# Seven block products in chunks 1 to 12 of a squared-ReLU MLP, with buffers of their own for the weights of its two products

## The chip, the cores and the metric

One core of one Trainium2 chip runs the whole program. The metric is the device time of one execution in microseconds (us); lower is better. A profile is one execution of its own, taken by the hardware profiler, with its own time beside its span. Engines: PE is TensorE's matmuls, PEld its weight loads, DVE VectorE, ACT ScalarE, POOL GpSimd, SP SyncE, which here only issues DMAs.

## The reference

One layer of a causal decoder with 256 rows of 1024 features in float32: an RMSNorm and a joint input projection; a gated convolution branch and a sparse attention branch; cross attention over 256 memory tokens; an MLP with squared ReLU; a final RMSNorm. The part that matters here:

```
h = h + _cross_attention(_rmsnorm(h, norm_x_g[l]), _rmsnorm(mem, norm_mem_g[l]), wx_q[l], wx_kv[l], wx_o[l])
hf = _rmsnorm(h, norm_ffn_g[l]) @ w_ff1[l]          # (256, 1024) @ (1024, 4096)
h = h + jnp.square(jax.nn.relu(hf)) @ w_ff2[l]      # (256, 4096) @ (4096, 1024)
return _rmsnorm(h, norm_final_g)
```

## The kernel before

Every large product is made in three matmuls of a rounded float32 format: high part times high part, high times low, low times high. So each weight block that arrives by DMA is split: ScalarE copies it to its high part (`hi`), VectorE subtracts that from the block and writes the low part (`lo`). The same is done with the activations.

The MLP runs over 16 chunks of 256 hidden features. For chunk i, f1 (`first`, line 1256) makes the hidden values in two halves of 128 features, each 24 matmuls of 256 columns, or, in the wide form, 8 of 512 and 8 of 256. The ReLU and the square follow on ScalarE, then the hidden rows are split into `fs` (its high and low parts), the stationary side of f2. In the program, chunk c's f2 stands with chunk c+2's f1: half of f1, half of f2, the other half of f1, the rest of f2. Chunks 0 to 12 (JOINED is 13) are accumulated in common banks; the last three make their products at the very end, row half by row half.

A chunk's f2 is a 2x2 block product: two row halves of 128 and two halves of the 256 features by two halves of the 1024 columns. It takes eight block products of three 512-wide matmuls each, or, in the chunks listed in SEVEN (line 60), seven: then sums of the weight quarters (`sums`) and differences of the hidden quarters (`fn`) are needed. The weight side has four parts: `left`, `last`, `outer`, `inner`. VectorE makes the sums and all the low parts. The f1 that stands beside chunk c's f2 is wide if c isn't listed, chunk 5 excepted, and so is the f1 of chunks 0 and 1.

The order on each engine is that of the program text; nothing is reordered. A few queues in the program set it: `high_jobs` holds the splits still to come, in the order of use; `split_high` (ScalarE's copy) and `split_low` (VectorE's subtraction) take the next one each time a weight is used, at most HALVES (6) ahead. Generators (`activation`, the row turning) go one step further at each `tick`. Weights are loaded by SP in the order of STREAM (line 34), each 1 MB block into the next of three `raw` buffers. `load` is called when the last low part of a block is written, so the three buffers serve f1 and f2 in turn. In four f1 chunks (BY_HALVES) the load is issued as two halves. Between the loads SP also issues 16 copies that turn the residual from features to rows (`h_rm`).

The names that the prediction's steps touch: `load` (line 164), `seven` (line 214), `split_high` and `split_low` (lines 273 to 285), `activation` (line 1164), `Hidden` (line 1195), `seventh` and `first` (lines 1250 to 1264). The helper at line 80 records all matmuls and all VectorE instructions, so the names of the tiles tell them apart.

Of the kernel before, what the change touches and what calls it, by code (L numbers as in the profile page):

```python
# [59 lines left out]
SEVEN = (2, 3, 4, 6, 7, 8, 9, 10, 11, 12)  # L60
JOINED = 13
BY_HALVES = tuple(("f1", i) for i in (4, 5, 6, 7))
# [52 lines left out]
def block_kernel(ctx, tc, x, xt, mem, memt, wst, wki, vecs, convw, gout, out):  # L115
# [45 lines left out]
    nload = [0]  # L161
    high_jobs, low_jobs = [], []

    def load(parts=1):
        if nload[0] >= len(STREAM):
            return
        c = nload[0]
        nload[0] += 1
        key = STREAM[c]
        raw = t8(f"raw{c}", F32, (P, N_CHUNK)) if c in EARLY else raws.tile([P, N_CHUNK], F32, tag="raw", name=f"raw{c}")  # L170
        n = KT * NK if key[0] == "ki" else N_CHUNK
        parts = 2 if key in BY_HALVES else parts
        src = wki if key[0] == "ki" else wst[INDEX[key]]
        for q in range(parts):
            ns = slice(q * n // parts, (q + 1) * n // parts)
            nc.sync.dma_start(raw[:, ns], src[:, ns])
        if key in WHOLE:
            whole[key] = raw.rearrange("p (k n) -> p k n", k=2 * KT)
            return
        if key[0] == "f2" and key[1] in SEVEN:  # L180
# [8 lines left out]
        if key[0] == "f2" and key[1] < JOINED:

            at = [j.key for j in high_jobs].index(("f1", key[1] + 2, 1))
            first = len(jobs) // 2
            high_jobs[at:at] = jobs[:first]
            jobs = jobs[first:]
        if key == ("f1", JOINED + 2):

            at = [j.key for j in high_jobs].index(("f2", JOINED - 1, "inner"))
            high_jobs[at:at] = jobs[:1]
            jobs = jobs[1:]
        high_jobs.extend(jobs)  # L200
# [12 lines left out]

    def seven(key, c, raw):

        b = raw.rearrange("p (k h n) -> p k h n", k=2, h=2)
        flat = raw.rearrange("p (j n) -> p j n", j=4)
        sums = []

        def outer():  # L220
            sums.append(t8(f"sums{c}", F32, (P, 4, 512)))
            dve.tensor_tensor(out=sums[0][:, 0:2, :], in0=flat[:, 0:4:3, :],
                              in1=flat[:, 1:2, :].to_broadcast([P, 2, 512]), op=ALU.add)

        def inner():
# [4 lines left out]
        def stage(name, src_of, n, before=None):  # L230
            def high():
                src = src_of()
                if before:
# [16 lines left out]
            return Stage((*key, name), high, before, not before)  # L250

        return [stage("left", lambda: b[:, :, 0, :], 2), stage("last", lambda: flat[:, 3:4, :], 1),
                stage("outer", lambda: sums[0][:, 0:2, :], 2, outer), stage("inner", lambda: sums[0][:, 2:4, :], 2, inner)]

    def high(key, c, raw, ns, q, last):
        n = ns.stop - ns.start
# [183 lines left out]
    zero_r = cst.tile([P, 512], F32R, name="zero_r")  # L440
# [9 lines left out]
    ki2 = cst.tile([P, S], F32, name="ki2")  # L450
# [191 lines left out]
    bias = [cst.tile([P, P * (qb + 1)], F32, name=f"bias{qb}") for qb in range(2)]  # L642
# [22 lines left out]
    def index_scores():  # L665
# [497 lines left out]

    def activation(c, ct, ps, t, sh, sl):
        if ps.shape[1] == S:
            act(t[:, ct, :], ps, AF.Relu)  # L1166
        else:
            yield from merge(t[:, ct, :], ps)
            yield
            act(t[:, ct, :], t[:, ct, :], AF.Relu)  # L1170
# [272 lines left out]
```

## Time and profile before

| | |
|---|---|
| time, median of 3 runs | 505.51 us (505.5 to 505.59) |
| the profiled execution's own time | 505.25 us |
| its span | 503.5 us |
| granted TensorE clock | 0.998 |
| PE busy | 493.6 us |
| DVE busy | 459.9 us |
| ACT busy | 349.1 us |
| f1 of chunk 0 begins | 323.05 us |
| last product begins to end | 480.6 to 497.3 us |

A line of the timeline gives start, duration, engine, line of the program, operation, tiles written and read, shape, and in brackets the idle time just before it and who ended it. Durations of VectorE's and ScalarE's instructions overlap their successors' a little, and matmuls are pipelined, so the cost of one in a row of many is read from start to start. In a line of the waits stand the total, the number and the longest.

### The profile page before, as it was taken

The page shows a single profiled execution, that of the slowest core. Times are in us where ns is not written, and L with a number is a line of the kernel's source. Part 1 is how long each engine was busy: PE and PEld are TensorE (multiplying, and loading weights), DVE is VectorE, ACT ScalarE, POOL GpSimd, SP SyncE. Part 2 cuts the span into 40 slices and gives each one's busy share as a digit, 9 for nine tenths or more (in the row PEclk, how much of TensorE's full clock was granted, in tenths as well). Part 3 has the DMA queues.
Part 4 walks back from the last instruction along what each step waited for, and adds up shares of the span by engine and source line. Part 5 has one row for each costly group of instructions (what it writes and reads, how often), then busy time and mean ns, then how long its engine had stood idle before and what let it go on. Part 6 is the DMA issues. An engine that isn't in the chain of part 4 may idle for free.

```text
span 503.5 us, 8292 instructions
## 1 busy us (share of the span) xinstructions
PE 493.6 (98%) x3119; PEld 444.1 (88%) x3119; DVE 459.9 (91%) x858; ACT 349.1 (69%) x639; POOL 31.6 (6%) x49
## 2 busy tenths in 40 slices
PE   7999999999999999999999999999999999999995
PEld 5999998888888888888889999988989899988984
DVE  5999999999999799999988986888999899999994
ACT  7657777788656676668756667586777677777832
POOL 2002212221021100000000000000000000000000
PEclk9999999999999999999999999999999999999999
DMA  8949678899787744345645454368855645544602
GB/s 312 381 184 280 185 191 261 226 246 262 225 265 215 191 148 144 119 158 197 246 169 218 175 174 161 127 192 214 239 181 184 235 159 206 221 178 168 251 1 84
DMA packets 27225, 100.36 MB, mean 199 GB/s; under 512 B 10656, under 2 KB 11552, under 8 KB 17200
## 3 DMA queue, kind: packets, MB, share of 16 engines
q1 hardware_dynamic: 23120, 92.90, 53.4%
q0 software_dynamic: 3632, 6.59, 7.3%
q8 instruction: 24, 0.39, 0.3%
q10 hardware_dynamic: 432, 0.33, 0.2%
q14 instruction: 17, 0.14, 0.1%
HBM read 91.16 MB, written 1.05 MB: 183 GB/s over the span
## 4 chain that ended last, share of the span: by engine, by line
PE 62%; DVE 18%; ACT 7%; DMA 7%; issue 5%; POOLq 0%; POOL 0%; DVEq 0%; ACTq 0%
PE ps_conv L80 10%; DMA raw<-in_wst_dram 6%; PE ps_f L80 6%; DVE lo L80 5%; PE ps_ao L80 4%; PE ps_q L80 4%; PE ps_k L80 4%; PE ps_ga L80 4%; PE ps_gc L80 4%; PE ps_v L80 4%; PE ps_xo L80 3%; DVE sums L80 3%; PE ps_qi L80 2%; PE ps_xk L80 2%; PE ps_p L80 2%
## 5 line engine op out<-in xcount | busy, mean ns | idle before, releaser
L80 DVE TENSOR_TENSOR lo<-raw,hi 128x1024 fp32r<-128x1024 f32 x141 | 170.5, 1214 | 5.2 <-ACT hi L263 5.1
L263 ACT ACTIVATE hi<-raw 128x1024 fp32r<-128x1024 f32 x141 | 146.7, 1046 | 2.0 <-DMA raw<-in_wst_dram 2.0
L80 PE MATMUL ps_f<-ff_p,hi 128*128 128x256 f32 (+1 forms) x448 | 92.8, 299 | 0.6 <-ACT ft L1166 0.3
L80 DVE SCALAR_TENSOR_TENSOR acc<-u,cw,acc 128x234 f32<-128x234 f32 (+29 forms) x190 | 78.0, 461 | 0.3
L80 PEld LDWEIGHTS ps_f<-ff_p,hi 128*128 128x128 f32 x448 | 72.8, 191 | 5.8 <-ACT ft L1166 2.0
L80 PE MATMUL ps_f<-ff_p,lo 128*128 128x256 f32 x256 | 70.9, 282 | 0.0
L80 PEld LDWEIGHTS ps_f<-ff_p,lo 128*128 128x128 f32 x256 | 48.8, 191 | 0.6
L80 PE MATMUL ps_conv<-n_p,hi 128*128 128x256 f32 x224 | 41.0, 285 | 0.0
L80 PEld LDWEIGHTS ps_conv<-n_p,hi 128*128 128x128 f32 x224 | 34.9, 192 | 0.8 <-issue 0.7
L80 PE MATMUL ps_conv<-n_p,lo 128*128 128x256 f32 x112 | 31.7, 283 | 0.0
L588 POOL DMA_DIRECT2D acc<-products x25 | 21.6, 864 | 125.1 <-ACT products L587 50.1
L80 PE MATMUL ps_p<-hi,fs 128*128 128x512 f32 (+1 forms) x88 | 27.2, 372 | 0.0
L80 PE MATMUL ps_q<-n_p,hi 128*128 128x512 f32 x64 | 23.6, 406 | 0.0
L80 PE MATMUL ps_k<-n_p,hi 128*128 128x512 f32 x64 | 23.5, 407 | 0.0
L80 PE MATMUL ps_ao<-o_p,hi 128*128 128x512 f32 x64 | 22.6, 401 | 0.0
L80 PE MATMUL ps_co<-u_p,hi 128*128 128x512 f32 (+1 forms) x80 | 22.2, 351 | 0.0
L80 PE MATMUL ps_mix<-mix_p,hi 128*128 128x512 f32 (+1 forms) x80 | 22.2, 351 | 0.0
L80 PE MATMUL ps_ga<-n_p,hi 128*128 128x512 f32 x64 | 22.0, 396 | 0.0
L80 PE MATMUL ps_gc<-n_p,hi 128*128 128x512 f32 x64 | 22.0, 396 | 0.0
L587 ACT ACTIVATE products<-u,cw 128x231 f32<-128x231 f32 (+24 forms) x50 | 21.9, 489 | 0.0
L80 PEld LDWEIGHTS ps_conv<-n_p,lo 128*128 128x128 f32 x112 | 21.5, 192 | 0.0
L80 PE MATMUL ps_v<-hi,n_p 128*128 128x512 f32 x64 | 19.9, 389 | 0.0
(386 smaller groups left out, 1215.8 us busy)
## 6 DMA issues: line engine op xcount, KB each, us to landing
raw<-in_wst_dram SPq DMA_DIRECT2D x76, 1024.0 KB, 4.9
acc<-products POOLq DMA_DIRECT2D x25, 256.0 KB, 5.3
raw<-in_wst_dram SPq DMA_DIRECT2D x12, 512.0 KB, 7.6
x_rm<-in_x_dram SPq DMA_DIRECT2D x2, 512.0 KB, 4.2
mem_rm<-in_mem_dram SPq DMA_DIRECT2D x1, 1024.0 KB, 8.9
mem_t<-in_memt_dram SPq DMA_DIRECT2D x1, 1024.0 KB, 10.9
h_t<-in_xt_dram SPq DMA_DIRECT2D x1, 1024.0 KB, 7.0
h_rm<-turned SPq DMA_DIRECT2D x16, 64.0 KB, 5.6
```

The source lines that it names most:

```text
L80: return fn(*args, **kwargs)
L263: act(hi, raw[:, ns], AF.Copy)
L587: act(prod[:, a, s:], u[:, t, : S - s], AF.Copy, scale=cw[:, t, TAPS - 1 - s : TAPS - s])
L588: nc.gpsimd.dma_start(acc[:, ts, :], prod, accum_op=ALU.add)
```

## The change

- SEVEN now holds chunks 1 to 12: chunks 1 and 5 go from eight to seven block products, and with chunk 1 the f1 of chunk 3 goes from the wide form to the narrow one. Chunk 0 keeps eight.
- From chunk 2 on, f1's weights have one buffer of their own (that of f1 of chunk 2), refilled by halves: when the low part of one half is written, the same half of the next chunk is fetched. f1 of chunk 3 has a buffer elsewhere and is fetched ahead. f2's blocks have the other two `raw` buffers; one is released after the last of its sums, not after its last low part.
- The splits' order is laid down once, ahead (`last_jobs`), and a split that uses a block that was not fetched yet waits for a later turn (`here`). The sums are made one instruction at a time (`step`).
- In chunks 1 to 14 the activation squares both halves at once, and splits all seven hidden parts with one copy and one subtraction of 128x896 (chunks 13 and 14: four parts, 128x512). The differences are made in other combinations, and the row halves change places, so that the seven parts lie in a row. The residual's and the output's row halves follow.
- Small tiles share memory (`picked`, `zero_r`) to make room for the larger activation tile.

```
-SEVEN = (2, 3, 4, 6, 7, 8, 9, 10, 11, 12)
+SEVEN = (1, 2, 3, 4, 5, 6, 7, 8, 9, 10, 11, 12)
+FIRST = STREAM.index(("f1", 2))
-BY_HALVES = tuple(("f1", i) for i in (4, 5, 6, 7))
+BY_HALVES = ()
...
+    order = [c for c, key in enumerate(STREAM) if key[0] != "f1" or key[1] < 3]
...
+    def release(key, c, q, last):
+
+        if key[0] == "f1" and key[1] > 1:
+            i = 4 if key[1] == 2 else key[1] + 1
+            if key[1] != 3 and i < 16:
+                fetch(STREAM.index(("f1", i)), raw_of[FIRST], 2, q)
+        elif last and c not in early:
+            load()
...
+        def inner(j):
             t = sums[0]
-            dve.tensor_tensor(out=t[:, 2, :], in0=t[:, 1, :], in1=flat[:, 0, :], op=ALU.add)
-            dve.tensor_tensor(out=t[:, 3, :], in0=t[:, 2, :], in1=flat[:, 2, :], op=ALU.add)
+            dve.tensor_tensor(out=t[:, j, :], in0=t[:, j - 1, :], in1=flat()[:, 2 * j - 4, :], op=ALU.add)
+            if j == 3:
+                release(key, c, 1, True)
...
+    fetch(STREAM.index(("f1", 3)), t8("raw_f1", F32, (P, N_CHUNK)))
...
+    def part(c, t, js, sh, sl):
+        act(sh[:, js, :], t, AF.Copy)
+        yield
+        dve.tensor_tensor(out=sl[:, js, :], in0=t, in1=sh[:, js, :].bitcast(F32), op=ALU.subtract)
...
     def activation(c, ct, ps, t, sh, sl):
+        if c in (0, 15):
+            yield from by_halves(c, ct, ps, t, sh, sl)
+            return
+        yield from relu(ps, t[:, 2 * ct : 2 * ct + 2, :].rearrange("p r n -> p (r n)"))
+        if ct == 0:
+            return
+        act(t[:, 0:4, :], t[:, 0:4, :], AF.Square)
+        yield
+        js = slice(0, 4)
+        if c in SEVEN:
+
+            dve.tensor_tensor(out=t[:, 4:6, :], in0=t[:, 0:1, :].to_broadcast([P, 2, P]), in1=t[:, 1:3, :], op=ALU.subtract)
+            yield
+            dve.tensor_tensor(out=t[:, 6, :], in0=t[:, 1, :], in1=t[:, 5, :], op=ALU.subtract)
+            yield
+            dve.tensor_tensor(out=t[:, 7, :], in0=t[:, 3, :], in1=t[:, 6, :], op=ALU.subtract)
+            yield
+            js = slice(1, 8)
...
+        yield from part(c, t[:, js, :], slice(0, js.stop - js.start), sh, sl)
```

Three places show what moves. First TensorE, in the first part of chunk 5's f2 (weight block 64, hidden rows `fs5`, accumulators `ps_p`). Before:

```order
L80 MATMUL ps_p2_3890<-hi64_0_4376,fs5_4214 128x512
L80 MATMUL ps_p2_3890<-lo64_0_4377,fs5_4214 128x512
L80 MATMUL ps_p2_3890<-hi64_0_4376,fs5_4214 128x512
L80 MATMUL ps_p4_3894<-hi64_0_4376,fs5_4214 128x512
L80 MATMUL ps_p4_3894<-lo64_0_4377,fs5_4214 128x512
L80 MATMUL ps_p4_3894<-hi64_0_4376,fs5_4214 128x512
L80 MATMUL ps_p3_3914<-hi64_0_4376,fs5_4214 128x512
L80 MATMUL ps_p3_3914<-lo64_0_4377,fs5_4214 128x512
L80 MATMUL ps_p3_3914<-hi64_0_4376,fs5_4214 128x512
L80 MATMUL ps_p5_3918<-hi64_0_4376,fs5_4214 128x512
L80 MATMUL ps_p5_3918<-lo64_0_4377,fs5_4214 128x512
L80 MATMUL ps_p5_3918<-hi64_0_4376,fs5_4214 128x512
```

and with the change:

```order
L81 MATMUL ps_p1_4007<-hi64left_4358,fs5_4202 128x512
L81 MATMUL ps_p1_4007<-lo64left_4359,fs5_4202 128x512
L81 MATMUL ps_p1_4007<-hi64left_4358,fs5_4202 128x512
L81 MATMUL ps_p2_3897<-hi64left_4358,fs5_4202 128x512
L81 MATMUL ps_p2_3897<-lo64left_4359,fs5_4202 128x512
L81 MATMUL ps_p2_3897<-hi64left_4358,fs5_4202 128x512
L81 MATMUL ps_p3_3907<-hi64last_4369,fs5_4202 128x512
L81 MATMUL ps_p3_3907<-lo64last_4370,fs5_4202 128x512
L81 MATMUL ps_p3_3907<-hi64last_4369,fs5_4202 128x512
```

Nine matmuls (`left` twice three, `last` three) stand where twelve did; the second part of the chunk has twelve in both.

Second VectorE, over one chunk in the middle (f2 block 70 is prepared). `lo_0` and `lo_1` are f1's halves, `ft` hidden rows, `fn` their differences. Before:

```order
L80 TENSOR_TENSOR sums_4642<-sums_4642,raw_4531 128x512 x2
L80 TENSOR_TENSOR fs_4555<-ft_4556,fs_4555 128x256
L80 TENSOR_TENSOR fs_4555<-fn_4653,fs_4555 128x512
L80 TENSOR_TENSOR outer_4664<-sums_4642,outer_4664 128x1024
L80 TENSOR_TENSOR inner_4678<-sums_4642,inner_4678 128x1024
L80 TENSOR_TENSOR lo_0_4710<-raw_4590,hi_0_4709 128x1024
L80 TENSOR_TENSOR fs_4674<-ft_4675,fs_4674 128x128
L80 TENSOR_TENSOR lo70left<-raw_4660,hi70left 128x1024
L80 TENSOR_TENSOR lo70last<-raw_4660,hi70last 128x512
L80 TENSOR_TENSOR sums_4759<-raw_4660 128x1024
L80 TENSOR_TENSOR fn_4770<-ft_4675 128x256
L80 TENSOR_TENSOR fn_4770<-ft_4675,fn_4770 128x128 x2
```

and now, at the like place:

```order
L81 TENSOR_TENSOR sums_4589<-sums_4589,raw_4413 128x512
L81 TENSOR_TENSOR ft_4536<-ft_4536 128x128
L81 TENSOR_TENSOR outer_4637<-sums_4589,outer_4637 128x1024
L81 TENSOR_TENSOR ft_4536<-ft_4536 128x128
L81 TENSOR_TENSOR inner_4650<-sums_4589,inner_4650 128x1024
L81 TENSOR_TENSOR lo_0_4680<-raw_3546,hi_0_4679 128x1024
L81 TENSOR_TENSOR fs_4535<-ft_4536,fs_4535 128x896
L81 TENSOR_TENSOR lo70left<-raw_4524,hi70left 128x1024
L81 TENSOR_TENSOR sums_4700<-raw_4524 128x1024
L81 TENSOR_TENSOR lo70last<-raw_4524,hi70last 128x512
L81 TENSOR_TENSOR sums_4700<-sums_4700,raw_4524 128x512
L81 TENSOR_TENSOR ft_4647<-ft_4647 128x256
```

The three subtractions that wrote `fs` are one of 896 elements, the two sums that depend on each other stand apart, and the differences are made between larger instructions.

Third SP, from the load of f1 of chunk 2 on. Before:

```order
L176 DMA raw_3550<-in_wst_dram 128x2048
L176 DMA raw_3604<-in_wst_dram 128x2048
L1137 DMA g_out_3713<-in_gout_dram 128x512
L1137 DMA g_out_3714<-in_gout_dram 128x512
L176 DMA raw_3741<-in_wst_dram 128x2048
L1158 DMA h_rm<-turned 32x16x32 x3
L176 DMA raw_3839<-in_wst_dram 128x2048
L1158 DMA h_rm<-turned 32x16x32 x2
L176 DMA raw_3880<-in_wst_dram 128x1024 x2
L1158 DMA h_rm<-turned 32x16x32 x3
L176 DMA raw_3952<-in_wst_dram 128x2048
L1158 DMA h_rm<-turned 32x16x32
```

and now (`raw_f` is f1 of chunk 3, `raw_3546` the buffer of f1, with halves of 128x1024):

```order
L178 DMA raw_3546<-in_wst_dram 128x2048
L178 DMA raw_3600<-in_wst_dram 128x2048
L1174 DMA g_out_3709<-in_gout_dram 128x512
L1174 DMA g_out_3710<-in_gout_dram 128x512
L178 DMA raw_f_3713<-in_wst_dram 128x2048
L178 DMA raw_3739<-in_wst_dram 128x2048
L1196 DMA h_rm<-turned 32x16x32
L178 DMA raw_3546<-in_wst_dram 128x1024
L1196 DMA h_rm<-turned 32x16x32 x2
L178 DMA raw_3546<-in_wst_dram 128x1024
L1196 DMA h_rm<-turned 32x16x32 x4
L178 DMA raw_3888<-in_wst_dram 128x2048
```

f1 of chunk 3 no longer waits for a buffer of the ring, f2 of chunk 1 takes its place there, and the halves of f1 follow one at a time.

More of the change, by code (lines that the diff above doesn't have):

```diff
@@ L160, in block_kernel, with fetch @@
     prepared, whole, elsewhere = {}, {}, set()
-    nload = [0]
+    order = [c for c, key in enumerate(STREAM) if key[0] != "f1" or key[1] < 3]
+    early = set(EARLY)
+    raw_of, landed = {}, set()
     high_jobs, low_jobs = [], []
[L164 to L168, printed above, removed]
+    def fetch(c, raw, parts=1, only=None):
         key = STREAM[c]
-        raw = t8(f"raw{c}", F32, (P, N_CHUNK)) if c in EARLY else raws.tile([P, N_CHUNK], F32, tag="raw", name=f"raw{c}")
@@ L189, in load @@
[L189 to L200, printed above, removed]
+            if only in (None, q):
+                ns = slice(q * n // parts, (q + 1) * n // parts)
+                nc.sync.dma_start(raw[:, ns], src[:, ns])
@@ new lines, in fetch, with load @@
+        raw_of[c] = raw
+        landed.update((key, q) for q in ((0, 1) if only is None else (only,)))
+    def load(parts=1):
+        if not order:
+            return
+        c = order.pop(0)
+        key = STREAM[c]
+        fetch(c, t8(f"raw{c}", F32, (P, N_CHUNK)) if c in early else raws.tile([P, N_CHUNK], F32, tag="raw", name=f"raw{c}"),
+              2 if key in BY_HALVES else parts)
+        if key in WHOLE:
+            whole[key] = raw_of[c].rearrange("p (k n) -> p k n", k=2 * KT)
+        elif c < FIRST:
+            high_jobs.extend(jobs_of(c))
+        elif c == FIRST:
+            high_jobs.extend(last_jobs())
@@ L244, in low, with high @@
                     prepared[(*key, name)] = (hi, lo)
-                    if name == "inner":
-                        load()
                 low_jobs.append(low)
[L250 to L256, printed above, removed]
+            return Stage((*key, name), high, steps, not steps, (key, 0))
+        return [stage("left", lambda: b()[:, :, 0, :], 2), stage("last", lambda: flat()[:, 3:4, :], 1),
+                stage("outer", lambda: sums[0][:, 0:2, :], 2, (outer,)),
+                stage("inner", lambda: sums[0][:, 2:4, :], 2, (lambda: inner(2), lambda: inner(3)))]
+    def high(key, c, ns, q, last):
+        raw, n = raw_of[c], ns.stop - ns.start
         if (*key, q) in elsewhere:
@@ L282, in split_low @@
             low_jobs.pop(0)()
-        if len(high_jobs) > 1:
-            high_jobs[1].prepare()
+        for job in high_jobs[:3]:
+            if job.steps and job.here():
+                job.step()
+                break
     nsplit, nused, held = [0], [0], [1]
@@ L1209, in row @@
         def row(self, k, rb):
[L1210 removed]
+            return self.of(2 * k + 1 - rb)
         def done(self):
```

148 lines of the change are left out of this document (76 added, 72 removed).

## The prediction

> **What bounds the kernel now.** I read the page first for the share of each engine, then the busy time by stage, then TensorE and VectorE in order of time, then the waits. From the page:
>
> ```profile
> PE 493.6 (98%) x3119; PEld 444.1 (88%) x3119; DVE 459.9 (91%) x858; ACT 349.1 (69%) x639; POOL 31.6 (6%) x49
> ```
>
> TensorE is busy 98% of the span, so only two things can shorten the time: fewer matmuls, or fewer of the short gaps between them. The change touches the MLP, so I cut it at the first f1 matmul of each chunk. The columns are the stretch, its length, busy time of PE, PEld, DVE, ACT and POOL (instructions), granted clock, DMA share, GB/s. The rows are chunks 1, 3, 5, 7, 10 and 11:
>
> ```profile
> 345.50:356.61 11.11, 11.11 (x58) 9.41 (x56) 9.10 (x15) 7.53 (x14) 0.00 (x0) 1.00 0.85 221
> ...
> 367.17:378.29 11.12, 10.83 (x71) 9.62 (x69) 11.02 (x16) 8.13 (x14) 0.00 (x0) 1.00 0.55 188
> ...
> 388.85:400.48 11.63, 11.50 (x73) 10.18 (x72) 9.75 (x14) 7.22 (x13) 0.00 (x0) 1.00 0.50 188
> ...
> 411.04:421.60 10.56, 10.56 (x70) 9.70 (x69) 10.38 (x15) 7.79 (x13) 0.00 (x0) 1.00 0.53 200
> ...
> 442.72:453.31 10.59, 10.59 (x70) 9.62 (x69) 10.48 (x16) 8.01 (x13) 0.00 (x0) 1.00 0.52 198
> 453.31:464.28 10.97, 10.84 (x71) 9.62 (x70) 10.87 (x16) 8.11 (x13) 0.00 (x0) 1.00 0.52 192
> ```
>
> An undisturbed chunk of seven products takes 10.56 us (chunk 7). Chunks 3, 10 and 11 are such chunks too, and take 0.56, 0.03 and 0.41 more. Chunks 1 and 5 are the ones with eight products. VectorE is nearly full from chunk 7 on. Its instructions over one such chunk, start, duration, name:
>
> ```profile
> 411.71 1.41 DVE L80 TENSOR_TENSOR sums<-sums,raw 128x512 f32<-128x512 f32 x2
> 413.04 0.42 DVE L80 TENSOR_TENSOR fs<-ft,fs 128x256 fp32r<-128x256 f32 x1
> 413.37 0.69 DVE L80 TENSOR_TENSOR fs<-fn,fs 128x512 fp32r<-128x512 f32 x1
> 413.98 1.22 DVE L80 TENSOR_TENSOR outer<-sums,outer 128x1024 fp32r<-128x1024 f32 x1
> 415.11 1.22 DVE L80 TENSOR_TENSOR inner<-sums,inner 128x1024 fp32r<-128x1024 f32 x1
> 416.25 1.22 DVE L80 TENSOR_TENSOR lo<-raw,hi 128x1024 fp32r<-128x1024 f32 x1
> 417.38 0.28 DVE L80 TENSOR_TENSOR fs<-ft,fs 128x128 fp32r<-128x128 f32 x1
> 417.75 1.23 DVE L80 TENSOR_TENSOR lo70left<-raw,hi70left 128x1024 fp32r<-128x1024 f32 x1
> 418.89 0.69 DVE L80 TENSOR_TENSOR lo70last<-raw,hi70last 128x512 fp32r<-128x512 f32 x1
> 419.49 1.22 DVE L80 TENSOR_TENSOR sums<-raw 128x1024 f32<-128x1024 f32 x1
> 420.62 0.42 DVE L80 TENSOR_TENSOR fn<-ft 128x256 f32<-128x256 f32 x1
> 421.08 0.62 DVE L80 TENSOR_TENSOR fn<-ft,fn 128x128 f32<-128x128 f32 x2
> 421.62 1.22 DVE L80 TENSOR_TENSOR lo<-raw,hi 128x1024 fp32r<-128x1024 f32 x1
> ```
>
> The next chunk's sums start at 422.75, 1.13 after the last row, so VectorE needs 11.04 us where TensorE needs 10.56. It loses 0.48 a chunk, and chunks 1 and 5, with less work for it, let it recover. Of what keeps it and ScalarE waiting, from MLP start to end:
>
> ```profile
> ACT inner L240 <- DVE sums L80: 8.0, 9, 1.2
> ACT hi66left L240 <- DMA raw<-in_wst_dram: 2.3, 1, 2.3
> PEld ps_f L80 <- ACT ft L1166: 2.0, 4, 0.7
> ```
>
> The four waits of the weight load for the ReLU go with the gaps of chunks 3, 5, 10 and 11. ScalarE is late with a ReLU because the instruction in front waits for VectorE's sums or for a load, and the accumulator that the next f1 half wants is not free. The gap of chunk 3 on TensorE:
>
> ```profile
> 371.88 0.39 PE L80 MATMUL ps_p<-hi60last,fs 128*128 128x512 f32 x1
> 372.56 0.50 PE L80 MATMUL ps_f<-ff_p,hi 128*128 128x256 f32 x2 [0.29 <-ACT ft L1166]
> ```
>
> **The change part by part.** First, the products. Twelve 512-wide matmuls (six of `outer`, and behind them six of `inner`) take from 364.42 to 367.17, thus 0.229 each:
>
> ```profile
> 364.42 1.55 PE L80 MATMUL ps_p<-outer,fs 128*128 128x512 f32 x6
> ...
> 367.17 0.40 PE L80 MATMUL ps_f<-ff_p,hi 128*128 128x256 f32 x2
> ```
>
> Chunk 5 loses one product of three matmuls: -0.69. The rest of its excess, 11.63 - 10.56 - 0.69 = 0.38, is its gap. Chunk 1 becomes an ordinary chunk: 11.11 to 10.56 = -0.55 (its f1 goes from two wide matmuls per tile to three narrow ones, which gives a little back and is contained in that difference). Bounds: these follow from counts, and I give them 0.05 either way. The Trainium skill ("TensorE: Matmul & The Clock Gate", Back-to-back issue gap) has about 131 ns for each 512-wide matmul in a sustained stream; by that the three would be worth 0.39 and the sum 0.3 smaller, but the rows here measure 0.229.
>
> Second, VectorE's chunk. By starts, a 128x1024 takes 1.13 (415.11 to 416.25), a 128x512 0.60 (418.89 to 419.49), a 128x256 0.33 (413.04 to 413.37) or 0.46 if the next one reads it (420.62 to 421.08), a dependent 128x128 0.27 (half of 421.08 to 421.62). The new chunk has six of 1024 (6.78), `last` (0.60), two sums now apart from one another (1.20), one 256 (0.33), two 128 (0.54), and one 128x896 in place of the three low parts. No row has 896 elements; between 512 and 1024 it is worth 0.60 to 1.13, and by the line through both, 1.00, nearest to the upper. Sum 10.45, with every reading at its worst (0.46 for the 256, 0.69 for each of the sums, 1.13) 10.89, at its best (a 128 at 0.20, a 256's 0.33 less a quarter of the 0.53 between 512 and 1024, and the 896 at 0.60) 9.91. I take 10.45: VectorE falls under TensorE's 10.56 even with the sums in every chunk. ScalarE merges the two squares and three copies of a chunk into one each and had room already (7.8 to 8.2 of 10.56).
>
> Third, the loads. Before, one ring of three buffers serves f1 and f2 and a load is issued at the end of VectorE's work on a buffer. Landing times of the weights (min/median/max) in 336 to 366 and in 400 to 440, then from the page the half loads of the whole program and ScalarE's copy of a half:
>
> ```profile
> DMA to landing us min/median/max: 4.0/7.3/8.8
> DMA to landing us min/median/max: 4.7/7.0/7.3
> raw<-in_wst_dram SPq DMA_DIRECT2D x12, 512.0 KB, 7.6
> L263 ACT ACTIVATE hi<-raw 128x1024 fp32r<-128x1024 f32 x141 | 146.7, 1046 | 2.0 <-DMA raw<-in_wst_dram 2.0
> ```
>
> Now f1 of chunk 3 is loaded ahead, right behind the two g_out loads. Each f2 block gets its buffer released before the last subtraction of its chunk and is read 1.5 chunks later (some 15 us, against 8.8), so its load is hidden. The f1 buffer is refilled by halves: a half is issued when its own low part is done and read by ScalarE one chunk on. With 1.05 for the copy and 1.22 for the subtraction, the landing may take 10.56 - 2.27 = 8.3 us before the loop is longer than TensorE's chunk. A half alone in the queue cannot be slower than a whole block alone (4.0 to 4.7 at best), so I price this at nothing; the cover is 3.6 us, and if it went, each microsecond over 8.3 would cost one per chunk. SP gets two rows more; each waits for VectorE in VectorE's own order, so none holds up a later load. The row copies (h_rm) keep their places or come earlier.
>
> With the ring and VectorE's debt gone, what made the four gaps is gone: -(0.56 + 0.38 + 0.03 + 0.41) = -1.38. Bounds: 0 to -1.38. I take all of it.
>
> Fourth, chunk 0. Its activation now squares chunk 1's hidden rows in one piece ahead of the copy of its own differences. After f1 of chunk 2 ends, ScalarE has copy, ReLU, square of 512 and copy in front of the product that needs the last:
>
> ```profile
> 336.52 0.40 ACT L1170 ACTIVATE ft<-ft 128x256 f32<-128x256 f32 x1
> 332.84 0.62 ACT L896 ACTIVATE sq_ff<-h_t 128x512 f32<-128x512 f32 x1
> 336.20 0.42 ACT L1190 ACTIVATE fs<-fn 128x256 fp32r<-128x256 f32 x1 [0.15 <-DVE fn L80]
> 338.16 0.50 PE L80 MATMUL ps_ff<-onesd,sums_ff 128*128 128x2 f32 x4
> ```
>
> That is about 0.4 + 0.4 + 0.6 + 0.4 = 1.8 us, while TensorE has the four small matmuls (338.16 to 338.52, 0.36) and six products (1.37), 1.73. I add +0.1; bounds 0 and the largest gap seen, 0.56. In chunks 0 and 1 VectorE gets about 3 us more work (the seven products' sums and parts), but it has idle time there, most of it behind a load that is now issued earlier:
>
> ```profile
> 352.67 1.23 DVE L80 TENSOR_TENSOR lo58left<-raw,hi58left 128x1024 fp32r<-128x1024 f32 x1 [1.58 <-ACT hi58left L240]
> ```
>
> Going through its new order with these durations, the low parts are ready 2 to 4 us ahead of the matmuls, so nothing is added; without that cover a gap like chunk 3's comes, 0.5.
>
> Fifth, the end. The last products set the end, and what follows them is unchanged:
>
> ```profile
> 486.62 0.68 DVE L80 TENSOR_TENSOR comb<-ps_p,comb 128x512 f32<-128x512 f32 x1
> 492.87 0.28 PE L80 MATMUL ps_p<-hi,fs 128*128 128x256 f32 x1
> 496.46 0.88 PE L80 MATMUL ps_p<-both,fs 128*128 128x256 f32 x6
> 497.38 0.48 DVE L80 SCALAR_TENSOR_TENSOR h_rm<-ps_p,ms_ff,h_rm 128x256 f32<-128x256 f32 x1 [1.21 <-PE ps_p L80]
> ```
>
> VectorE frees the last accumulators at 487.3, over 5 us ahead of TensorE's use of them, and the change brings VectorE forward as well, so TensorE does not run into it. Swapped row halves and the shared small tiles move no wait ahead of the MLP: 0.
>
> **Sum:** -0.69 - 0.55 - 1.38 + 0.10 = -2.52. The profiled execution took 505.25 (span 503.5 and 1.75 around it), so 502.7; the median shown is 505.51, 0.26 more, so 503.0.
>
> **Rivals.** (A) The refill of the single f1 buffer takes the place of the old waits. If halves land as late as the worst landing above, 8.8, the loop is 8.8 + 2.27 = 11.07 and each of twelve chunks grows by 0.51: +6.1, thus 503.0 + 6.1 = 509.1, slower. It decides from a landing of 8.3 us; a mean of 8.6 already cancels the gain. For it: the median of 7.6 for half loads. Against: those twelve were issued in pairs, the second of a pair behind the first, and now each half stands alone. The Trainium skill ("DMA: Bandwidth & Descriptors", Bandwidth) says to batch transfers to 1 MiB or more, which speaks against halving; by its fit of 2.0 us plus bytes over 436 GB/s (Anatomy of one DMA) a half would take an estimated 3.2 us, so the halving would cost rate and not this loop. Chance 0.07.
>
> (B) VectorE stays the bound. At 10.89 it loses 0.33 a chunk. Before, losing 0.48 a chunk, it went from chunk 6 to 11 until the gap of 0.41, so its lead is about 2.4 us, gone after seven chunks; the other five lose 0.33 each, 1.65, where 0.44 (chunks 10, 11) was lost before. Sum -0.69 - 0.55 - 0.94 (the gaps of chunks 3 and 5) + 0.10 + (1.65 - 0.44) = -0.87 on 505.51: 504.6. For it: 99% busy now. Against: three small steps are merged. Chance 0.10.
>
> (C) The early chunks pay: VectorE has no light chunk 1 any more and gaps as in chunk 3 (0.56) come in two of chunks 0 to 2: 503.0 + 1.1 = 504.1. Chance 0.10.
>
> (D) The change does not do it: the gaps stay for a reason other than VectorE and loads, and only the counts act: 505.51 - 1.24 = 504.3. Chance 0.05.
>
> **How the numbers follow.** The forecast (502.5 to 503.6) has 0.68. A difference of 0.2% (1.0 us, from 504.5 to 506.5) is what a measurement of this kernel tells from none. Forecast, C, D and a part of B lie below 504.5: 0.83. No change: half of B and small forms of A, 0.10. Slower: the rest of A, 0.07. The range for eight in ten goes from the sum with no chunk-0 gap and 0.3 for the counts and the spread, 502.6, to B's 504.6.
>
> **What would show it.** Right: chunks 1 to 11 all at 10.56 by TensorE, no wait of the weight load for a ReLU there, VectorE with some idle time in each chunk, no wait of ScalarE's copies for loads after chunk 3, and 21 product matmuls in each of chunks 1 to 12. Wrong: chunks above 10.6 with ScalarE waiting for the f1 load (A), VectorE at 10.5 or more per chunk and gaps late in the row (B), gaps before 370 (C). The 128x896 subtraction near 1.1 in duration would confirm its price.

## The result, and the profile after

| | before | changed |
|---|---|---|
| time, median of 6 runs each on one chip | 505.55 us (505.3 to 505.85) | 503.15 us (503.08 to 503.55) |
| the profiled execution's own time | 505.25 us | 503.16 us |
| its span | 503.5 us | 501.0 us |
| first f1 matmul to the last f1 half of the MLP | 322.82 to 477.73, 154.91 us | 322.74 to 475.36, 152.62 us |
| last six matmuls of the last products begin | 496.46 us | 494.10 us |

The ratio is 0.995, 95% interval 0.9937 to 0.9962: the changed kernel is 2.4 us faster, where 2.5 was forecast. (The first f1 matmul of the kernel before starts at 322.82; the 323.05 in the table ahead of the prediction is the start of the second.) The chunks show where it comes from. These are the windows of chunks 1, 2, 6, 10 and 11 of the changed kernel, cut and with the columns as in the prediction:

```profile
345.75:356.30 10.55, 10.55 (x70) 9.70 (x69) 10.16 (x14) 8.64 (x13) 0.00 (x0) 1.00 0.67 180
356.30:366.86 10.56, 10.56 (x70) 9.70 (x69) 10.56 (x14) 7.33 (x11) 0.00 (x0) 1.00 0.67 210
398.54:409.10 10.56, 10.56 (x70) 9.69 (x69) 10.56 (x14) 7.50 (x11) 0.00 (x0) 1.00 0.55 199
440.78:451.34 10.56, 10.56 (x70) 9.70 (x69) 10.45 (x14) 7.61 (x11) 0.00 (x0) 1.00 0.58 199
451.34:461.90 10.56, 10.56 (x70) 9.70 (x69) 9.95 (x12) 7.61 (x12) 0.00 (x0) 1.00 0.59 201
```

Every chunk takes TensorE's 10.56, and TensorE (second number after the window) is busy all of it: the gaps are gone. VectorE (fourth) has no idle time at all in chunks 2 to 9, of which 2 and 6 are shown; the prediction did not expect that. Its chunk now, from `sums` to `sums`, with the rows between left out:

```profile
406.78 1.25 DVE L81 TENSOR_TENSOR sums<-raw 128x1024 f32<-128x1024 f32 x1
...
411.19 0.31 DVE L81 TENSOR_TENSOR ft<-ft 128x128 f32<-128x128 f32 x1
411.39 1.25 DVE L81 TENSOR_TENSOR outer<-sums,outer 128x1024 fp32r<-128x1024 f32 x1
...
415.00 1.12 DVE L81 TENSOR_TENSOR fs<-ft,fs 128x896 fp32r<-128x896 f32 x1
416.00 1.25 DVE L81 TENSOR_TENSOR lo70left<-raw,hi70left 128x1024 fp32r<-128x1024 f32 x1
417.14 1.25 DVE L81 TENSOR_TENSOR sums<-raw 128x1024 f32<-128x1024 f32 x1
```

417.14 - 406.78 = 10.36 us, 0.20 less than TensorE's chunk. So VectorE enters chunk 2 late and catches up 0.2 a chunk; in chunk 10 it has idle time again. ScalarE's wait for the sums shows the same (first, fourth and tenth of ten rows): it stands at 2.21 in the second to the fourth row and then falls by about 0.2 a row to 1.29 in the ninth. The waits of the MLP hold no more wait of the weight load for a ReLU:

```profile
359.53 1.06 ACT L275 ACTIVATE inner<-sums 128x1024 fp32r<-128x1024 f32 x1 [2.70 <-DVE sums L81]
360.49 0.37 ACT L1204 ACTIVATE ft<-ps_f 128x256 f32<-128x256 f32 x1
...
390.61 1.06 ACT L275 ACTIVATE inner<-sums 128x1024 fp32r<-128x1024 f32 x1 [2.21 <-DVE sums L81]
...
453.03 1.06 ACT L275 ACTIVATE inner<-sums 128x1024 fp32r<-128x1024 f32 x1 [1.29 <-DVE sums L81]
```

```profile
ACT inner L275 <- DVE sums L81: 19.1, 11, 2.7
ACT ft L1204 <- PE ps_f L81: 14.8, 18, 1.4
```

The first of ScalarE's waits, the 2.70, is close to costing time. The ReLU behind the wait ends at 360.49 + 0.37 = 360.86, and TensorE wants its accumulator at 361.24:

```profile
361.24 0.40 PE L81 MATMUL ps_f<-ff_p,hi 128*128 128x256 f32 x2
```

That is 0.38 us of cover (a chunk later it is 0.58: the ReLU ends at 371.22, TensorE begins at 371.80), and the experiments below show that there is not much more.

### The profile page after: what moved, and what is told of

It reads as the page before. It is cut to its first block, busy times and chain, and to the rows that moved or that the text cites. A ratio compares the mean times of both kernels' runs of the same rounds, so it can differ in the third digit from the quotient of the medians.

```text
span 501.0 us, 8293 instructions
## 1 busy us (share of the span) xinstructions
PE 491.7 (98%) x3129; PEld 443.9 (89%) x3129; DVE 463.4 (92%) x844; ACT 345.6 (69%) x601; POOL 31.7 (6%) x49
## 4 chain that ended last, share of the span: by engine, by line
PE 84%; DVE 8%; ACT 3%; issue 2%; DMA 1%; POOL 0%; POOLq 0%; SPq 0%; DVEq 0%; ACTq 0%
PE ps_f L81 18%; PE ps_p L81 12%; PE ps_conv L81 10%; PE ps_ao L81 4%; PE ps_q L81 4%; PE ps_k L81 4%; PE ps_ga L81 4%; PE ps_gc L81 4%; PE ps_v L81 4%; PE ps_xo L81 3%; PE ps_qi L81 2%; PE ps_xk L81 2%; PE ps_xv L81 2%; DVE lo L81 2%; PE ps_xq L81 2%
## 5 line engine op out<-in xcount | busy, mean ns | idle before, releaser
L81 DVE TENSOR_TENSOR lo<-raw,hi 128x1024 fp32r<-128x1024 f32 x135 | 164.1, 1219 | 4.5 <-ACT hi L297 4.2
L297 ACT ACTIVATE hi<-raw 128x1024 fp32r<-128x1024 f32 x135 | 140.5, 1046 | 1.2 <-DMA raw<-in_wst_dram 1.2
L81 PEld LDWEIGHTS ps_f<-ff_p,hi 128*128 128x128 f32 x464 | 75.3, 191 | 3.7
L275 ACT ACTIVATE inner<-sums 128x1024 fp32r<-128x1024 f32 x12 | 12.7, 1061 | 19.1 <-DVE sums L81 19.1
L1204 ACT ACTIVATE ft<-ps_f 128x256 f32<-128x256 f32 x26 | 9.8, 379 | 14.8 <-PE ps_f L81 14.8
```

Of the source, the lines that this page charges most:

```text
L81: return fn(*args, **kwargs)
L275: act(hi, src, AF.Copy)
L297: act(hi, raw[:, ns], AF.Copy)
L1204: act(t, ps, AF.Relu)
```

## The experiments

The table gives for each kernel the median, the ratio to the kernel before (measured beside it) with its 95% interval, the stretch from the first f1 matmul to the last f1 half of the MLP in the profiled execution, and, by TensorE's rows, those of chunks 1 to 11 that are not 10.56 us long. Chunk 0 (22.68 before, 23.00 changed) and chunk 12 (9.20 in both) are named where they stand out. The stretch is the steadiest measure: the work ahead of it is the same, but its begin varies between programs by up to 0.5 us (322.64 to 323.15).

| kernel | median us | ratio (interval) | stretch us | chunks over 10.56 us |
|---|---|---|---|---|
| before | 505.55 | 1 | 154.91 | 1: 11.11, 3: 11.12, 5: 11.63, 10: 10.59, 11: 10.96 |
| changed | 503.15 | 0.995 (0.9937 to 0.9962) | 152.62 | none |
| old_list | 504.43 | 0.9983 (0.9974 to 0.9992) | 153.86 | 1: 11.11, 5: 11.24 |
| before_seven | 511.06 | 1.0111 (1.0097 to 1.0124) | 160.98 | 2: 15.10, 3: 10.66, 4 to 10: 11.04 on average, 11: 11.21 |
| old_ring | 508.2 | 1.0055 (1.0042 to 1.0068) | 157.67 | 2: 11.22, 3: 10.93, 4 to 10: 11.01 on average, 11: 10.94, 12: 9.57 |
| old_act | 506.83 | 1.0029 (1.0018 to 1.004) | 156.54 | 2: 14.62, 11: 10.73 |
| old_act_eight | 503.17 | 0.9952 (0.9934 to 0.9971) | 152.87 | 1: 11.10, 11: 10.59 |
| three_parts | 503.58 | 0.9959 (0.9945 to 0.9972) | 152.62 | none |
| diff_twice | 506.33 | 1.0022 (1.0013 to 1.0031) | 155.76 | 0: 23.43, 2: 10.79, 3 to 11: 10.81 to 10.95 |
| last_twice | 509.25 | 1.0079 (1.0066 to 1.0091) | 158.62 | 2: 11.30, 3 to 11: 11.08 to 11.09, 12: 9.60 |
| whole_refill | 503.22 | 0.996 (0.9946 to 0.9974) | 152.62 | none |
| whole_load | 534.08 | 1.0558 (1.0528 to 1.0588) | 183.70 | 2: 11.15, 3 to 11: 13.02 to 13.19, 12: 16.89 |
| fetch_twice | 543.44 | 1.0746 (1.0716 to 1.0776) | 193.55 | 2: 10.80, 3 to 11: 13.4 to 15.8, 12: 18.78 |
| fix0 | 502.67 | 0.9948 (0.9935 to 0.9962) | 152.35 | none |

**The counts alone: old_list.**

```
-SEVEN = (1, 2, 3, 4, 5, 6, 7, 8, 9, 10, 11, 12)
+SEVEN = (2, 3, 4, 6, 7, 8, 9, 10, 11, 12)
```

> The changed kernel, but chunks 1 and 5 keep eight block products (the list of SEVEN is the old one). Theory: the gaps of chunks 3, 5, 10 and 11 (1.38 us before) are gone because VectorE and the loads keep up, whatever chunks 1 and 5 do; only the counts come back: 0.69 + 0.55 = 1.24 us, so 503.15 + 1.24 = 504.4, and chunks 2 to 4 and 6 to 11 at 10.56 us each. Rival (the four gaps hang on the two chunks with eight products, for instance on their wide f1): gaps of about 1.4 us come back with them, 505.8.

The stretch grows by 153.86 - 152.62 = 1.24 us, 0.55 in chunk 1 and 0.68 in chunk 5. No gap comes with them. The counts are worth what the prediction said, and the gaps do not hang on the eight products.

**The list without the rest: before_seven.** The same line, the other way, in the kernel before.

> The kernel before with the new list alone: chunks 1 and 5 as seven block products, with the old shared ring and the old activation. Theory: VectorE needs 11.04 us a chunk against TensorE's 10.56 and now has no chunk to recover in. With a lead of about 2.4 us it is used up after five chunks, and the other chunks lose 0.48 each: gaps of 3.4 to 4.0 us in place of 1.38, so 505.55 - 1.24 + 2.0 to 2.6 = 506.3 to 506.9, slower than before. Rival (the counts are what the change is worth, rings and activation do nothing): 505.55 - 1.24 = 504.3.

5.5 us slower than before, where 0.8 to 1.4 was expected. Chunk 2 alone loses 4.54 us, and from chunk 4 on a chunk takes 11.04. The steady loss is as expected: VectorE's chunk is 10.95 to 11.20 there, nearly without a wait. The early loss is not: TensorE waits for a ReLU until 363.80, which costs 2.93 us, and its matmuls then run at a granted clock of 0.67 for 4.5 us, which costs the other 1.61. Twelve chunks of seven do not fit in the old rings with the old activation.

**The old ring: old_ring.** Three edits: all blocks in `order`, `release` always calls `load`, no fetch ahead.

```
-    order = [c for c, key in enumerate(STREAM) if key[0] != "f1" or key[1] < 3]
+    order = list(range(len(STREAM)))
...
-        if key[0] == "f1" and key[1] > 1:
...
-        elif last and c not in early:
+        if last and c not in early:
...
-    fetch(STREAM.index(("f1", 3)), t8("raw_f1", F32, (P, N_CHUNK)))
```

> The changed kernel, but all weight blocks of both products go in turn through one ring of three buffers again, f1 whole in 1 MB loads and nothing fetched ahead; list, order of splits and activation stay as changed. Theory (VectorE's time made the gaps, the loads came second): a ring turn is two blocks in 10.56, so each of three buffers has 15.8 us for a landing of about 7 and a hold of about 7.6 us; it just fits, 503.2 to 503.7. Rival (the shared ring's loads made the gaps): waits of ScalarE's copies for loads and gaps of 1 us or more in all, 504.5 or slower.

The rival was right about this kernel: 508.2, about 0.45 us lost in each chunk from 2 to 11. The loop can be read off. The load of the next f2 block is issued at the end of f1's second low part; ScalarE's copy waits for it; VectorE waits for that copy. SP, ScalarE and VectorE of this kernel over one turn:

```profile
404.08 0.33 SPq L178 DMA_DIRECT2D raw<-in_wst_dram  x1
415.04 0.33 SPq L178 DMA_DIRECT2D raw<-in_wst_dram  x1
```

```profile
408.88 1.06 ACT L271 ACTIVATE hi68left<-raw 128x1024 fp32r<-128x1024 f32 x1 [1.07 <-DMA raw<-in_wst_dram]
```

```profile
409.98 1.23 DVE L81 TENSOR_TENSOR lo68left<-raw,hi68left 128x1024 fp32r<-128x1024 f32 x1 [0.51 <-ACT hi68left L271]
...
413.80 1.22 DVE L81 TENSOR_TENSOR lo<-raw,hi 128x1024 fp32r<-128x1024 f32 x1
```

408.88 - 404.08 = 4.80 for the load, 409.98 - 408.88 = 1.10 for the copy, 415.04 - 409.98 = 5.06 for VectorE's work until the next load: 10.96 us. What I counted, 15.8 us for a landing and a hold, left out that the turn goes through VectorE in the order of its instructions. VectorE's own work is little changed here (10.96 - 0.51 = 10.45), and it is the wait of 0.51 in each turn that makes its chunk longer than TensorE's.

**The old activation: old_act and old_act_eight.** In the changed kernel, `activation`, `Hidden.t`, the row halves and TERMS as before. In the second run chunk 1 also keeps eight products:

```
-SEVEN = (1, 2, 3, 4, 5, 6, 7, 8, 9, 10, 11, 12)
+SEVEN = (2, 3, 4, 5, 6, 7, 8, 9, 10, 11, 12)
```

> The changed kernel with the activation as before (squares by halves, three copies and three subtractions for the seven parts, the old differences and row halves); list, rings and single sums stay as changed. VectorE's chunk by the rows: six of 1.13, 0.60, two sums of 0.60, 0.33 + 0.60 + 0.20 to 0.27 for the parts, 0.33 to 0.46 and 0.54 for the differences, together 10.6 to 10.8 us against 10.56. Theory: it loses 0.05 to 0.25 a chunk, 0.6 to 2.6 us over eleven chunks, about the lead; chunk 0 gets its 0.25 back: 502.9 to 503.6. Rival (merging the activation is what takes VectorE off the path): back to 0.4 us and more lost per chunk, 505 or slower.

> The changed rings and single sums with the old activation, and chunk 1 with eight products. With chunk 1 as seven this kernel lost 2.5 and 1.6 us in chunks 2 and 3 and nothing to speak of later. Theory (VectorE is behind in chunk 2 because chunk 1's sums and parts come on top of what it still has from chunk 0): without them chunks 2 and 3 lose 0.5 us at most together, so 506.83 - 4.06 + 0.55 (chunk 1's ninth to twelfth products' share of the count) + 0 to 0.5 = 503.3 to 504.0. Rival (the old activation itself needs that time whenever f1 goes narrow): the gaps stay, 507.

Neither theory of the first run holds: 506.83, but not by 0.4 a chunk. All but 0.2 of the loss, 4.06 us, lies in chunk 2 (the second expectation gives part of it to chunk 3), and chunks 3 to 10 are at 10.56. ScalarE and TensorE there:

```profile
360.32 0.63 ACT L1228 ACTIVATE fs<-fn 128x512 fp32r<-128x512 f32 x1 [3.44 <-DVE fn L81]
...
363.02 0.37 ACT L1204 ACTIVATE ft<-ps_f 128x256 f32<-128x256 f32 x1
```

```profile
363.44 0.50 PE L81 MATMUL ps_f<-ff_p,hi 128*128 128x256 f32 x2 [2.31 <-ACT ft L1204]
```

ScalarE's copy of the differences stands ahead of the ReLU and waits 3.44 us, because VectorE has not come to the differences yet. In the changed kernel the copy of the parts stands behind that ReLU. Part of VectorE's lateness comes from the same order one chunk earlier: there the like copy waits 1.80 us, `inner` behind it comes late, and VectorE itself waits 1.24 us for that (0.39 in the changed kernel).

The pause is only 2.47 of the 4.06 us. The other 1.59 come right behind it. The first row is the f1 half after the pause in old_act, the second the same half in the changed kernel, up to the first product:

```profile
363.44:367.90 4.46, 4.46 (x25) 4.46 (x25) 4.46 (x6) 3.01 (x5) 0.00 (x0) 0.62 0.99 315
```

```profile
361.24:364.11 2.87, 2.87 (x25) 2.86 (x24) 2.87 (x3) 2.87 (x4) 0.00 (x0) 1.00 0.98 358
```

The same matmuls take 4.46 us at a granted clock of 0.62 and 2.87 at 1.00. So this pause of TensorE cost more than the wait itself.

With chunk 1 at eight products the loss is gone: 503.17, the time of the changed kernel and a little under the expected 503.3 to 504.0, with the old activation. VectorE is not faster for it. Its rows one chunk apart in old_act_eight:

```profile
417.75 1.22 DVE L81 TENSOR_TENSOR sums<-raw 128x1024 f32<-128x1024 f32 x1
...
428.50 1.22 DVE L81 TENSOR_TENSOR sums<-raw 128x1024 f32<-128x1024 f32 x1
```

That is 10.75, 0.19 over TensorE's chunk, and the first gap comes in chunk 11, with 0.03. So a light chunk 1 gives VectorE a lead of at least 1.7 us (nine chunks of 0.19), and without it the same activation runs into the pause in chunk 2. The new activation is what lets chunk 1 have seven products. That is worth 0.55 us, of which 0.3 is given back in chunk 0 (below). The rest of the gain needs only the rings, the new order of the splits with the sums one at a time, and the list.

**Pieces or one: three_parts.**

```
-        yield from part(c, t[:, js, :], slice(0, js.stop - js.start), sh, sl)
+        cuts = ((1, 4), (4, 6), (6, 8)) if c in SEVEN else ((0, js.stop),)
+        lo = js.start
+        for a, b in cuts:
+            act(sh[:, a - lo : b - lo, :], t[:, a:b, :], AF.Copy)
+        yield
+        for a, b in cuts:
+            dve.tensor_tensor(out=sl[:, a - lo : b - lo, :], in0=t[:, a:b, :], ...
```

> The changed kernel with its differences and its order, but the seven hidden parts are copied and subtracted in three pieces (384, 256 and 256 columns) and not in one of 896. VectorE: 0.46 + 0.33 + 0.33 in place of 1.00, so 10.48 a chunk, still under 10.56. Theory (the old activation lost by its order: a copy of differences stood in ScalarE's queue before VectorE had come to them; pieces cost little): 503.2 to 503.6. Rival (it lost by the number of instructions, so that the merged copy and subtraction are what counts): 505 or slower.

The stretch is 152.62 us, as in the changed kernel; the 0.4 in the median lies ahead of it (its MLP begins at 323.15, the changed kernel's at 322.74). The merging of the copies and subtractions is worth nothing here. What is left between this run and old_act is mainly order: the squares in one piece, the differences one at a time between larger instructions, the copy behind the ReLU. Which of these counts most was not tried. The order also shortens VectorE's chunk, from 10.75 to 10.50, since a difference no longer stands right behind the one whose result it reads.

**How much cover: diff_twice and last_twice.** One VectorE instruction per chunk is made twice.

```
-            dve.tensor_tensor(out=t[:, 4:6, :], in0=t[:, 0:1, :].to_broadcast([P, 2, P]), ...
+            for _ in range(2):
+                dve.tensor_tensor(out=t[:, 4:6, :], in0=t[:, 0:1, :].to_broadcast([P, 2, P]), ...
```

```
-                    dve.tensor_tensor(out=lo, in0=src, in1=hi.bitcast(F32), op=ALU.subtract)
+                    for _ in range(2 if name == "last" else 1):
+                        dve.tensor_tensor(out=lo, in0=src, in1=hi.bitcast(F32), op=ALU.subtract)
```

> As the run before, with a smaller step: the first difference of the hidden quarters (128x256, 0.33 us more) is made twice. VectorE's chunk goes to 10.69, 0.13 over TensorE's. Theory (cover 0.38 us): gaps from chunk 3 or 4 on, 1.0 to 1.5 us in all, 504.2 to 504.7. Rival (lead of 2.4 us): eleven chunks lose 1.4 us, less than the lead, so no gap and 503.2.

> The changed kernel, but VectorE makes the low part of the weight part last twice in each chunk of seven (128x512, 0.60 us more; the second writes the same values). VectorE's chunk goes from 10.36 to 10.96, 0.40 over TensorE's 10.56. Theory now (the cover is thin: at 360.49 the ReLU behind the wait for VectorE's sums ends 0.38 us before TensorE needs its accumulator): nearly all of it shows, from chunk 2 on 0.40 a chunk, about 4.0 us, 507.2, as evenly as 10.96 a chunk. Rival (the lead of 2.4 us that the prediction took): 4.4 - 2.4 = 2.0 us, 505.2, with the first half of the chunks at 10.56.

Both are dearer than either theory said. A second instruction that writes the same tile waits for the first, so the steps are larger: of last_twice VectorE's rows a chunk apart, and between them the doubled one:

```profile
401.00 1.41 DVE L81 TENSOR_TENSOR lo66last<-raw,hi66last 128x512 fp32r<-128x512 f32 x2
402.33 0.69 DVE L81 TENSOR_TENSOR sums<-sums,raw 128x512 f32<-128x512 f32 x1
...
413.42 0.68 DVE L81 TENSOR_TENSOR sums<-sums,raw 128x512 f32<-128x512 f32 x1
```

The pair takes 1.33, so 0.73 more and not 0.60, and VectorE's chunk is 413.42 - 402.33 = 11.09 = 10.36 + 0.73. That is TensorE's chunk too, from 3 to 11. For diff_twice it is 10.83, near 10.36 + 0.46; this run also loses 0.43 in chunk 0, where TensorE's weight load waits for the `fs` that stands behind the doubled instruction. So above 10.56 the time follows VectorE one for one from chunk 2 on. With seven products in chunk 1 the lead of 2.4 us that the prediction worked with does not exist; 0.2 a chunk and a few tenths at the start are all there is. It was read from the kernel before, where chunk 5 is light, and old_act_eight shows such a lead behind a light chunk 1.

**The refill of f1: whole_refill, whole_load and fetch_twice.** First both halves fetched at the second low part, then the block in one load, then each half twice.

```
-            if key[1] != 3 and i < 16:
-                fetch(STREAM.index(("f1", i)), raw_of[FIRST], 2, q)
+            if key[1] != 3 and i < 16 and q == 1:
+                for q in range(2):
+                    fetch(STREAM.index(("f1", i)), raw_of[FIRST], 2, q)
```

> The changed kernel, but the one f1 buffer is refilled whole: both halves are fetched when the low part of the second half is written. Theory: the refill becomes a loop of landing 4.4, copy 1.05 and VectorE's work from the low part of the first half to that of the second, 7.4 us: about 12.9 us a chunk against 10.56, over eleven chunks 26 us, 523 to 533. Rival (the halves are a detail, since a refill has the rest of a chunk to land): within 1 us of 503.15.

> The refill by halves tried again: in the run before this the first half was still issued at its own low part, because a load waits only for the reads of the part that it overwrites and the queue stood idle ahead of it (loads at 394.48, 400.43 and 404.84, as in the changed kernel). Now f1's block is refilled with one 1 MB load, which must wait for both low parts. Theory: a loop of landing about 5.3, copy 1.05 and VectorE's work from the start of the first half's low part to the end of the second's, 7.2 us: 13.5 us a chunk against 10.56, 32 us over eleven chunks, 520 to 537. Rival (halves are a detail, ScalarE and VectorE can take the wait): within 1 us of 503.15.

The first of these changed nothing, for the reason that the second expectation gives: the place in the program does not hold a load back, only the reads that it waits for, and SP had nothing else to do. With one 1 MB load the loop is there. SP, ScalarE and VectorE of whole_load:

```profile
411.43 0.33 SPq L178 DMA_DIRECT2D raw<-in_wst_dram  x1
...
424.63 0.33 SPq L178 DMA_DIRECT2D raw<-in_wst_dram  x1
```

```profile
416.33 1.06 ACT L297 ACTIVATE hi<-raw 128x1024 fp32r<-128x1024 f32 x1 [2.96 <-DMA raw<-in_wst_dram]
```

```profile
417.42 1.23 DVE L81 TENSOR_TENSOR lo<-raw,hi 128x1024 fp32r<-128x1024 f32 x1 [2.74 <-ACT hi L297]
...
423.37 1.23 DVE L81 TENSOR_TENSOR lo<-raw,hi 128x1024 fp32r<-128x1024 f32 x1
```

4.90 for the landing, 1.09 for the copy, 7.21 from one low part to the end of the other: 13.20, where 13.5 was expected, and 534.08 us. This loop costs 23.4 us in chunks 2 to 11. Another 7.7 come in chunk 12, where TensorE waits 4.60 us for the ReLU behind a late block and then runs at a granted clock of 0.50 for 4.8 us. The loop alone thus gives 23.4 of the 32 us that were expected of it. Even so it shows that the refill by halves is what makes one f1 buffer enough. The Trainium skill ("DMA: Bandwidth & Descriptors", Bandwidth) says to batch transfers to 1 MiB or more; here two halves cost nothing and the single load 31 us, since the work that must be done before the next load can be issued decides, and not the rate.

> The changed kernel, but each half of f1's refill is fetched twice, the second fetch of the same bytes waiting for the first, so that a half lands about 9 us after the first issue and not 4.4. Theory (the limit of the prediction, 8.3 us): the loop is 9.2 + 1.05 + 1.22 = 11.5 us, 0.9 to 1.0 over TensorE's chunk, in about ten chunks: 511 to 514. Rival (the copies run far enough ahead that even this is hidden): 503.2.

The sign is right and the size is not: 13.4 us a chunk and more, where 11.5 was expected. The waits of SP's queue tell why:

```profile
SPq L178 <- DMA raw<-in_wst_dram: 97.4, 17, 8.3
```

SP waits for the first fetch before it can issue the second, 97.4 us in all, and every later load stands behind that wait. The run therefore delays all loads of the MLP and does not measure the limit of 8.3 us.

**Chunk 0 as before: fix0.** In `by_halves`, chunk 0's differences are made and copied together with the rows.

```
+        if c == 0 and ct:
+            dve.tensor_tensor(out=t[:, 4:6, :], in0=t[:, 1:4:2, :], in1=t[:, 0:4:2, :], op=ALU.subtract)
+            act(sh[:, js, :], t[:, js, :], AF.Copy)
+            act(sh[:, 4:6, :], t[:, 4:6, :], AF.Copy)
+            yield
+            for s in (js, slice(4, 6)):
+                dve.tensor_tensor(out=sl[:, s, :], in0=t[:, s, :], ...
+            return
         yield from part(c, t[:, js, :], js, sh, sl)
```

> The changed kernel with chunk 0's last steps in the order of before: the copy of its differences stands right behind the copy of its rows, ahead of the next accumulator's copy, ReLU and the 512-wide square. Theory: the 0.25 us that chunk 0 lost (its f2 to chunk 1's second f1 half takes 8.99 where it took 8.71) comes back and nothing else moves: 503.15 - 0.25 = 502.9, the span 0.25 shorter. Rival (the copy that is moved ahead delays the other copies by as much, and TensorE waits there instead): 503.15.

In the changed kernel the copy of the differences came at 338.21, behind ReLU and square, and TensorE's weight load waited for it:

```profile
337.67 0.63 ACT L1233 ACTIVATE ft<-ft 128x512 f32<-128x512 f32 x1
338.21 0.40 ACT L1211 ACTIVATE fs<-ft 128x256 fp32r<-128x256 f32 x1
338.66 0.19 PEld L81 LDWEIGHTS ps_p<-hi,fs 128*128 128x128 f32 x1 [0.35 <-ACT fs L1211]
```

With fix0 it comes 2 us earlier, and no wait is left:

```profile
336.21 0.42 ACT L1223 ACTIVATE fs<-ft 128x256 fp32r<-128x256 f32 x1 [0.15 <-DVE ft L81]
```

The stretch is 0.27 us shorter than the changed kernel's, all of it in chunk 0 (from the first f1 matmul to chunk 1: 22.73 against 23.00, and 22.68 before). Its median, 502.67, is the best of all kernels here. The two intervals overlap, so the times alone do not tell it from the changed kernel; the trace does.

## Why the prediction was right, and where it was not

- **The counts, -0.69 and -0.55: right.** old_list gives 0.68 and 0.55.
- **The gaps, -1.38: right in size, short in cause.** In the chunks of the changed kernel 0.56 + 0.38 + 0.03 + 0.40 are gone. The prediction put them down to VectorE's debt and the shared ring together, but worked only with the debt. The kernel before tells them apart. ScalarE and the weight load at the gaps of chunk 3 and chunk 5:

```profile
371.18 1.06 ACT L240 ACTIVATE inner<-sums 128x1024 fp32r<-128x1024 f32 x1 [0.88 <-DVE sums L80]
372.14 0.36 ACT L1166 ACTIVATE ft<-ps_f 128x256 f32<-128x256 f32 x1
372.56 0.30 PEld L80 LDWEIGHTS ps_f<-ff_p,hi 128*128 128x128 f32 x2 [0.71 <-ACT ft L1166]
...
393.38 1.06 ACT L240 ACTIVATE hi66left<-raw 128x1024 fp32r<-128x1024 f32 x1 [2.29 <-DMA raw<-in_wst_dram]
394.34 0.36 ACT L1166 ACTIVATE ft<-ps_f 128x256 f32<-128x256 f32 x1
394.76 0.30 PEld L80 LDWEIGHTS ps_f<-ff_p,hi 128*128 128x128 f32 x2 [0.55 <-ACT ft L1166]
```

  In chunk 3 the ReLU stands behind a copy that waits 0.88 us for VectorE's sums, and in chunks 10 and 11 it is the same (at 446.21 and 457.17, 0.88 each). In chunk 5 it stands behind a copy that waits 2.29 us for a load. So VectorE's sums stand behind 1.0 of the 1.38 and a load behind 0.38; and VectorE's lateness in chunk 3 has a load behind it too, the wait of 1.58 at 352.67 that the prediction shows. With chunk 1 at eight products the rings and the order of the splits alone take these gaps away, all but 0.03 (old_act_eight), although VectorE is still over TensorE's chunk. With seven, either of the old parts loses more than the gain: the ring by its loop of 10.96 us (old_ring), the old activation by its backlog in chunk 2 (old_act). The old ring with eight products in chunk 1 was not run with the rest changed.
- **VectorE's chunk, 10.45: measured 10.36.** The 128x896 subtraction takes 1.00 from start to start, as taken. The two 128x128 differences now stand apart and cost 0.20 each and not 0.27 (411.19 to 411.39), 0.14 less; the 128x1024 instructions, at 1.13 to 1.14, give a little of that back. The doubled instructions agree with the sum: 10.83 and 11.09.
- **The 0.2 us that are left do not show as idle time: wrong.** Up to chunk 9 VectorE spends them on catching up. Behind this is a wrong margin in the step on chunk 0: "the low parts are ready 2 to 4 us ahead" looked at the weights' low parts, while the tight chain is sums, copy of `inner`, ReLU, accumulator, with 0.38 us. Rival (C), early gaps, was therefore much nearer than its 0.10: 0.46 us more per chunk (diff_twice) is enough to open it, and the old activation paid 4.06 us in chunk 2. That the changed order leaves 0.38 us there was not worked out ahead; in this the forecast had luck.
- **The f1 refill, 0: right.** Landings in the middle of the MLP:

```profile
DMA to landing us min/median/max: 4.1/4.7/6.5
```

  All of them are under the 8.3 us of the prediction, and rival (A) did not come. The halves among them took 4.2 to 5.0 (the prediction's estimate from rate was 3.2), the whole blocks, each issued 0.6 us behind a half, 6.2 to 6.5. The 4.0 that the prediction read as a whole block's best was that of a half; a whole block alone took 4.7 at best, and the halves stay near that. That a loop through the f1 buffer can set the time, whole_load shows; the limit of 8.3 itself was not measured. (C) and (A) are the two ways in which this change could have failed, and the order of a few instructions and the halving kept it from that.
- **Chunk 0, +0.10: mis-sized.** It cost 23.00 - 22.68 = 0.32 us. The prediction had the right instructions but set their sum, 1.8, against TensorE's 1.73 as if both began together. ScalarE's first of them waits for the end of f1, and the weight load waits for the last of them.
- **The end, 0: right.** The last products begin 496.46 - 494.10 = 2.36 earlier, and the stretch up to the last f1 half is 2.29 shorter.

The sum by the trace is -1.24 - 1.37 + 0.32 = -2.29, where -2.52 was forecast; nearly all of the difference is chunk 0.

## What to carry to other kernels

When a stage is lengthened for one engine, look for the place where an in-order queue joins the engines (here ScalarE's ReLU behind a wait for VectorE) and measure the margin there in the first turns, not the average share: an average of 0.2 us to spare went with 0.38 us of cover in chunk 2, and where that cover was missing (old_act) the pause also lowered the granted clock. A buffer's loop is the landing plus all that the releasing engine has in its order between two releases; halving a buffer shortens that second part. And the order in two queues can be worth more than three instructions made into one: here 4.06 us in chunk 2 against nothing.

## What was not expected of the hardware

- VectorE's durations went up from 1.22 to 1.25 us for 128x1024 in the middle of the MLP, while the starts stayed 1.13 to 1.14 apart (416.00 to 417.14 above). For VectorE, which is full here, it is this spacing that adds up to the 10.36 of a chunk.
- A VectorE instruction that writes the tile that the one before it wrote starts later: 128x512 costs 0.73 in such a pair and 0.60 elsewhere, 128x256 0.46 and 0.33. Doubling an instruction is therefore not a dose of its plain price.
- A load that was moved to a later place in the program was not issued later. SP's queue was far enough ahead that the halves went out at 394.48, 400.43 and 404.84 in whole_refill, and at 394.42, 400.37 and 404.78 in the changed kernel, whose MLP begins 0.06 earlier.
- Behind most of its long pauses TensorE ran more slowly for some 4.5 us: at a granted clock of 0.62 behind 2.31 us in old_act, 0.67 behind 2.77 us in before_seven, 0.50 behind 4.60 us in whole_load. Pauses of up to 1.40 us in every chunk of whole_load left it at 1.00. The length alone does not decide, though: in fetch_twice it was 0.62 behind 2.12 us (374.32) and 1.00 behind 2.48 us (396.40). Why is open.
